# A transformer layer on one core: low weight halves without adding DMAs, modulation at a shorter interval, and one more raw weight buffer

## The chip, the cores and the metric

The kernel runs on one core of one Trainium2 chip. The metric is the device time of one execution in microseconds (us). The core's engines are TensorE (PE in the profile, its weight loads PEld), VectorE (DVE), ScalarE (ACT) and GpSimd (POOL); SyncE (SP) issues most DMAs. Each engine takes its instructions in program order and waits at each for semaphores of others.

## What is computed

One layer of a hybrid model over 512 tokens of width 2048, in float32. Cut to what matters here:

```python
mod = silu(c) @ w_ada + b_ada                      # 2048 x 12288
sh1, sc1, gt1, sh2, sc2, gt2 = split(mod, 6)
h = rms_norm(x, norm1_g) * (1 + sc1) + sh1
proj = h @ w_in                                    # attention and RWKV columns
att_out = dsa_sparse_attention(q, k, v, iq, ik, iw)    # index scores, top-k, softmax
rwkv_out = rwkv7_time_mix(...)                     # a scan over time with a 64 x 64 state per head
x = x + gt1 * (concat([att_out, rwkv_out]) @ w_out)
h2 = rms_norm(x, norm2_g) * (1 + sc2) + sh2
x = x + gt2 * ((silu(h2 @ w_ffn_gate) * (h2 @ w_ffn_up)) @ w_ffn_down)
```

## The kernel before, in words

**Big products.** Every product with a large weight matrix runs in float32r with operands that are split in two: `hi` is the value rounded to float32r, `lo` is what the rounding left. A product is three matmuls of 128 x 128 weights with 512 columns (hi x hi, hi x lo, lo x hi). The weights come in *jobs* (`job`, line 235): one job is one raw chunk `wraw` of up to 512 KB, usually four blocks of 128 rows by 256 columns, and 24 matmuls. Its matmuls write `acc` (or `vacc`) in PSUM.

**Weights on the way.** `issue_to` (line 242) issues the raw load of a job into one of three `wraw` buffers; `run_jobs` (line 272) calls it at the start of job i for the jobs up to i + 2. `split_to` (line 250) turns half a raw chunk at a time into a `whi` and a `wlo` tile of 128 x 512, four buffers of each. At the start of job i the halves of job i + 1 are split, in the middle the first half of job i + 2 may follow. There are two ways to split. The common one, `split` (line 196), is a cast on ScalarE for `whi` and a subtraction on VectorE for `wlo`. In the middle part of the program (`state["mid"]`, from the first job after the first block until the output product) every second half goes another way: the cast on ScalarE, then a second ScalarE instruction that writes -hi into `wlo`, then a DMA on GpSimd's queue that reads the same weights again from memory and adds them onto `wlo`.

**The order of the work.** The program is written by Python generators that run beside each other while the kernel is built. `run_jobs` is the main one; each time it yields, every other stream may write some instructions: the preparation of the RWKV pairs (`prep`, line 657), two triangular solves (`solve`, line 787; the first on GpSimd, the second on VectorE), two scans over time, the index scores and the top-k, the attention heads, and the modulation. A record of estimated engine times, `clk`, decides when a stream may go on: `until(tile)` waits for the estimated time at which a tile is ready, `room("dve", lim)` until VectorE's estimated backlog is at most `lim` us. So a number in such a call sets the order of instructions on all engines, and nothing else does.

**The modulation.** The first two sixths of `mod` are made at the start on TensorE. The other four (`gt1`, `sh2`, `sc2`, `gt2`) come from `ada_stream` (line 974): 16 blocks of 512 columns, each of 16 chunks `wad` of 128 x 512 (256 KB). A chunk is loaded by SP three chunks ahead into a tile of the general pool, and VectorE adds it, scaled, onto the block's sum in one instruction; the first chunk of a block is scaled by ScalarE. A block's sum is then reduced over partitions on VectorE (`ada_sum`, line 1010: a transpose and a reduce). A chunk may be worked on once `PACE` us (line 137) of the estimated time have gone by since the last and VectorE's backlog is under 2.0 us:

```python
            while now() < last + (PACE if bi < 12 else PACE2):
                yield
            yield from until(t)
            yield from room("dve", 2.0)
```

The first 12 blocks, 192 chunks, have to be done before the second norm: `norm2` (its first lines are `while done["ada"] < 12: yield`) writes nothing until then. Then it takes the sum of squares `ssum` through TensorE (`pst`), a power on GpSimd and TensorE's transposes (`prb`), and the first `h2` is made on VectorE and ScalarE. The FFN's products follow.

**The general pool.** `gpool` (line 166) has 29 tiles of 128 x 512 float32, 2 KB per partition each, for all the streams' work, the chunks `wad` included.

Nearly all instructions are recorded by one helper, so that the profile shows them at line 127.

Of the kernel before, what the change touches and what calls it, by code (L numbers as in the profile page):

```python
# [8 lines left out]
F32 = mybir.dt.float32  # L9
F32R = mybir.dt.float32r  # L10
I32 = mybir.dt.int32
AF = mybir.ActivationFunctionType
OP = mybir.AluOpType
# [10 lines left out]
PAIRS = 8  # L24
# [24 lines left out]
def layer_kernel(ctx, tc, x, c, positions, w_ada, b_ada, norm1_g, w_in, q_norm_g, k_norm_g,  # L49
# [38 lines left out]
    class Queue:  # L88
# [3 lines left out]
        def __getattr__(self, op):  # L92
# [3 lines left out]
            def call(*args, **kw):  # L96
# [26 lines left out]
                if key2 != "pe":  # L123
                    for v in vals[1:]:
                        if nm(v) in psread:
# [4 lines left out]
    PE, V, A, P, SP = (Queue(e, k) for e, k in ((nc.tensor, "pe"), (nc.vector, "dve"), (nc.scalar, "act"),  # L130
                                                (nc.gpsimd, "pool"), (nc.sync, "dma")))

    def now():
        return clk["pe"]

    SLACK = 0.5
    PACE, PACE2 = 4.2, 3.0

    def until(*aps):

        t = max(ready.get(nm(a), 0.0) for a in aps) + SLACK
        while now() < t:
            yield

    def room(key="dve", lim=3.0):
        while clk[key] - now() > lim:
            yield
# [15 lines left out]
    hpool = ctx.enter_context(tc.tile_pool(name="hp", bufs=32))  # L163
    wpool = ctx.enter_context(tc.tile_pool(name="wp", bufs=2))
    bpool = ctx.enter_context(tc.tile_pool(name="bp", bufs=6))
    gpool = ctx.enter_context(tc.tile_pool(name="gp", bufs=29))
    spool = ctx.enter_context(tc.tile_pool(name="sp", bufs=8))
    pgp = ctx.enter_context(tc.tile_pool(name="pg", bufs=4, space=PSUM))
    rpool = ctx.enter_context(tc.tile_pool(name="rp", bufs=8))
# [3 lines left out]
    def G(name="g", dt=F32):  # L173
        return gpool.tile([128, 512], dt, name=name, tag="g")
# [18 lines left out]
    def mm(o, l, r, start=True, stop=True):  # L193
        PE.matmul(o, l, r, start=start, stop=stop)

    def split(hi, lo, src, eng=None):
        A.copy(hi, src)
        (eng or V).tensor_tensor(lo, src, hi.bitcast(F32), op=OP.subtract)
# [34 lines left out]
    state = {"issued": 0, "split": 0, "mid": False, "ffn": False}  # L233
# [8 lines left out]
    def issue_to(n, eng=SP):  # L242
        while state["issued"] < min(n, len(jobs)):
            j = jobs[state["issued"]]
            t = wpool.tile([128, 1024], F32, name="wraw", tag="wraw", bufs=3)
            j["raw"] = t[:, 0:j["nk"] * j["n"]].rearrange("p (k m) -> p k m", m=j["n"])
            eng.dma_start(j["raw"], j["view"][:, j["k0"]:j["k0"] + j["nk"], j["c0"]:j["c0"] + j["n"]])
            state["issued"] += 1

    def split_to(n):  # L250
        while state["split"] < min(n, len(subs)):
            j, u = subs[state["split"]]
            if j["i"] >= state["issued"]:
                return
            h = max(1, j["nk"] // 2)
            hi = wpool.tile([128, 512], F32R, name="whi", tag="whi", bufs=4)
            lo = wpool.tile([128, 512], F32R, name="wlo", tag="wlo", bufs=4)
            hv, lv = (t[:, 0:h * j["n"]].rearrange("p (k m) -> p k m", m=j["n"]) for t in (hi, lo))
            if state["mid"] and state["split"] % 2:
                A.copy(hv, j["raw"][:, u * h:(u + 1) * h])  # L260
                A.activation(lv, hv.bitcast(F32), AF.Copy, scale=-1.0)
                P.dma_start(lv, j["view"][:, j["k0"] + u * h:j["k0"] + u * h + h, j["c0"]:j["c0"] + j["n"]],
                            accum_op=OP.add)
            else:
                split(hv, lv, j["raw"][:, u * h:(u + 1) * h])
            j["hi"] += [hv[:, i, :] for i in range(h)]
            j["lo"] += [lv[:, i, :] for i in range(h)]
            state["split"] += 1
# [3 lines left out]
    def run_jobs(a, b, eng=SP, every=3):  # L272
        for i in range(a, b):
            j = jobs[i]
            while j["need"] is not None and not j["need"]():
                yield
            if j["before"] is not None:
                j["before"]()
            issue_to(i + 3, eng)
            split_to(j["s0"] + 4)  # L280
            n = 0
            half = None
            for kk, o, l, r, st, sp in j["mms"](j):
                if half is None and j["nk"] > 1 and kk >= j["nk"] // 2 and not j["whole"]:
                    half = 1
                    split_to(j["s0"] + 5)
                mm(o, l, r, st, sp)
                n += 1
                if n % every == 0:
                    yield  # L290
            if j["after"] is not None:
                j["after"]()
# [63 lines left out]
    done = {"ada1": 0, "prep": 0, "idx": 0, "topk": 0, "ada": 0, "hfree": 0, "rb": 0}  # L356
# [7 lines left out]
    for k1, n1 in BLOCKS:  # L364
        for kind in ("scale", "shift"):
            n = 4 // n1
# [72 lines left out]
    def ccol(k):  # L439
        return cact[:, k:k + 1]  # L440
# [63 lines left out]


    issue_to(3, P)
    V.memset(vr2[:, 0:128], 0.0)
    for t in range(1, NT):
# [465 lines left out]
    def ada_stream():  # L974
        blocks = [(n, o, b) for n, o in (("gt1", 2), ("sh2", 3), ("sc2", 4), ("gt2", 5)) for b in range(4)]
        chunks = [(bi, k) for bi in range(16) for k in range(KD)]
        tiles = {}

        def load(i):
            if i < len(chunks):  # L980
                bi, k = chunks[i]
                n, o, b = blocks[bi]
                t = G("wad")
                SP.dma_start(t, wav[:, k, o * D + b * 512:o * D + b * 512 + 512])
                tiles[i] = t

        nl = 0
        acc = None
        last = 0.0
        for i, (bi, k) in enumerate(chunks):  # L990
            while bi >= 12 and not state["ffn"]:
                yield
            while nl < min(i + 3, 192 if bi < 12 else 256):
                load(nl)
                nl += 1
            t = tiles.pop(i)
            while now() < last + (PACE if bi < 12 else PACE2):
                yield
            yield from until(t)
            yield from room("dve", 2.0)  # L1000
            last = now()
            if k == 0:
                A.activation(t, t, AF.Copy, scale=ccol(0))
                acc = t
                continue
            V.scalar_tensor_tensor(acc, t, ccol(k), acc, op0=OP.mult, op1=OP.add)
            if k == KD - 1:
                start(ada_sum(acc, *blocks[bi]))

    def ada_sum(acc, n, o, b):  # L1010
        yield from until(acc)
        part = parts[o % 2]
        yield from room("dve", 4.0)
        colsum(part[:, b * 16:b * 16 + 16], acc)
        if b < 3:
            return
        yield from until(part)
        yield from banks(1)
        pc = PS("pc")
        spread(pc[:, 0:16], part)  # L1020
        yield
        V.tensor_tensor(mod[n], pc[:, 0:16], v1[:, o * 16:o * 16 + 16], op=OP.add)
        if n == "sc2":
            V.scalar_tensor_tensor(gp2, mod[n], 1.0, v1[:, 112:128], op0=OP.add, op1=OP.mult)
        done["ada"] += 4
# [215 lines left out]
    def start(gen):  # L1241
        streams.append(gen)
# [218 lines left out]
    ada_issue()  # L1461
    drive(until(jobs[1]["raw"]))
    split_to(4)

    def first_need(b):
# [3 lines left out]
    for b in range(len(BLOCKS)):  # L1469
        drive(first_need(b))  # L1470
        if b == 2:
            vectors2()
        drive(run_jobs(2 * b, 2 * b + 2, P if b < len(BLOCKS) - 1 else SP, 3))
# [15 lines left out]
    start(post_stream(range(0, 8, 2)))  # L1489
    start(post_stream(range(1, 8, 2)))  # L1490
    start(ada_stream())
    start(idx_stream())
    start(head_stream())
    start(head_stream())
    start(mixed_stream())
    state["mid"] = True
    drive(run_jobs(nfirst, i_out))
    state["mid"] = False
    drive(run_jobs(i_out, i_norm2))
    split_to(i_norm2 + 2)  # L1500
    drive(norm2())
# [63 lines left out]
```

## Time and profile before

| what | value |
|---|---|
| time, median of 3 runs | 2835.9 us (2832.57 to 2840.85) |
| the profiled execution | 2832.56 us, its span 2830.8 us |
| TensorE busy | 2678.4 us, 95% of the span, mean granted clock 0.970 |
| VectorE busy | 1396.9 us, 49% |
| ScalarE busy | 877.0 us, 31% |
| GpSimd busy | 438.1 us, 15% |
| DMA | 424.76 MB, mean 150 GB/s |

How to read it: the shares are means over parts with different limits. TensorE's granted clock is a share of full speed; its two levels are 2.4 GHz (1.0) and 1.2 GHz (0.5). A wait is named by the engine and the tile it was about to write, then by whom it waited for: "PE acc <- DMA wlo" is TensorE's product `acc` held up by a DMA into `wlo`. A wait for several semaphores is put down to the one that came last. Idle time counts for the end only where it holds up TensorE's chain.

### The profile page before, as it was taken

Reading aid. Unit: us, or ns where it says so; the run is one execution under the profiler, and the core shown is the slowest. Engines: PE = TensorE matmul, PEld = TensorE weight load, DVE = VectorE, ACT = ScalarE, POOL = GpSimd, SP = SyncE. Lnnn points to the kernel's source line nnn. Section 1 sums busy time; section 2 is a strip of 40 time slices with the busy share of each in tenths; the row PEclk is TensorE's granted clock in tenths of the full one; section 3 lists DMA queues with packets and bytes.
Section 4 is the critical chain, followed back from the end, with each engine's and each line's share of the span. In section 5 each row is a group of like instructions: output and inputs, shape, how many; then the busy total and the mean of one; then the engine's idle time right before and its main releaser. Section 6 shows DMA issues by size and latency. Waiting matters only on the chain.

```text
span 2830.8 us, 35243 instructions
## 1 busy us (share of the span) xinstructions
PE 2678.4 (95%) x13343; PEld 2116.4 (75%) x13343; DVE 1396.9 (49%) x2304; ACT 877.0 (31%) x1577; POOL 438.1 (15%) x455
## 2 busy tenths in 40 slices
PE   7989988879999979998699999999999999999999
PEld 4567766657777757887488888888888888888887
DVE  3455555778657876655854533332333323333233
ACT  3244433323332334432332222222222222222222
POOL 2012267851113323210300000000000000000000
PEclk8999999889999989999799999999999999999999
DMA  9987888587867546545454433323333333333333
GB/s 323 308 229 194 208 191 214 149 204 177 222 170 205 130 123 156 158 164 174 135 185 164 156 97 97 97 94 100 97 97 97 97 97 97 97 97 97 97 97 112
DMA packets 411963, 424.76 MB, mean 150 GB/s; under 512 B 55226, under 2 KB 359168, under 8 KB 411792
## 3 DMA queue, kind: packets, MB, share of 16 engines
q1 hardware_dynamic: 381312, 387.78, 44.2%
q0 software_dynamic: 30336, 34.46, 7.6%
q8 instruction: 105, 1.72, 0.2%
q14 instruction: 66, 0.54, 0.1%
q10 hardware_dynamic: 144, 0.26, 0.0%
HBM read 386.77 MB, written 35.65 MB: 149 GB/s over the span
## 4 chain that ended last, share of the span: by engine, by line
PE 79%; DMA 7%; DVE 5%; issue 4%; SPq 2%; ACT 1%; POOL 1%; POOLq 0%; DVEq 0%; ACTq 0%
PE acc L127 68%; DMA wlo<-in_w_in_dram 3%; PE vacc L127 3%; DMA wraw<-in_w_in_dram 2%; PE po L127 2%; SPq L127 2%; PE p L127 2%; PE adaacc L127 1%; DMA wada<-in_w_ada_dram 1%; DVE work L127 1%; PE pl L127 1%; DVE wlo L127 1%; DVE score L127 1%; PE dot L127 0%; DMA xtok<-in_x_dram 0%
## 5 line engine op out<-in xcount | busy, mean ns | idle before, releaser
L127 DVE TENSOR_TENSOR wlo<-wraw,whi 128x512 fp32r<-128x512 f32 (+2 forms) x750 | 517.5, 695 | 1106.8 <-ACT whi L127 1097.5
L127 ACT CAST whi<-wraw 128x512 fp32r<-128x512 f32 (+2 forms) x860 | 518.0, 608 | 1393.6 <-PE acc L127 1200.6
L127 PE MATMUL acc<-hhi,wlo 128*128 128x512 f32 (+1 forms) x2256 | 892.8, 396 | 51.1 <-DMA wlo<-in_w_in_dram 45.7
L127 PE MATMUL acc<-hhi,whi 128*128 128x512 f32 (+1 forms) x2256 | 915.5, 406 | 6.9 <-ACT hhi L127 3.9
L127 PE MATMUL acc<-hlo,whi 128*128 128x512 f32 (+1 forms) x2256 | 888.9, 394 | 3.4 <-DVE hlo L127 3.4
L127 PEld LDWEIGHTS acc<-hhi,wlo 128*128 128x128 f32 (+1 forms) x2256 | 428.3, 190 | 152.3 <-DMA wlo<-in_w_in_dram 52.8
L127 PEld LDWEIGHTS acc<-hhi,whi 128*128 128x128 f32 (+1 forms) x2256 | 428.2, 190 | 127.7 <-issue 28.8
L127 PEld LDWEIGHTS acc<-hlo,whi 128*128 128x128 f32 (+1 forms) x2256 | 428.4, 190 | 96.1 <-DVE hlo L127 6.2
L127 PE MATMUL acc<-act,whi 128*128 128x512 f32 x1408 | 434.9, 390 | 0.0
L127 PEld LDWEIGHTS acc<-act,whi 128*128 128x128 f32 x1408 | 263.2, 188 | 53.9
L127 PE MATMUL acc<-act,wlo 128*128 128x512 f32 x704 | 274.0, 389 | 0.0
L127 POOL DMA_DIRECT2D wlo<-in_w_in_dram x109 | 126.6, 1161 | 451.0 <-ACT wlo L127 359.2
L127 DVE SCALAR_TENSOR_TENSOR wad<-wad,cact 128x512 f32<-128x512 f32 x240 | 195.1, 813 | 1.2
L127 PEld LDWEIGHTS acc<-act,wlo 128*128 128x128 f32 x704 | 132.1, 188 | 27.6
L127 PE MATMUL acc<-mhi,whi 128*128 128x512 f32 x256 | 100.4, 392 | 0.0
L127 PE MATMUL acc<-mhi,wlo 128*128 128x512 f32 x256 | 99.7, 389 | 0.0
L127 PE MATMUL acc<-mlo,whi 128*128 128x512 f32 x256 | 99.6, 389 | 0.0
L127 DVE SCALAR_TENSOR_TENSOR x<-acc,gt,x 128x512 f32<-128x512 f32 x80 | 57.3, 751 | 39.8 <-PE acc L127 39.8
L127 POOL TENSOR_TENSOR stmp<-X,N 128x504 f32<-128x504 f32 (+33 forms) x69 | 71.1, 1031 | 3.3
L127 ACT ACTIVATE wlo<-whi 128x512 fp32r<-128x512 f32 (+1 forms) x110 | 69.2, 629 | 3.5
L127 POOL TENSOR_TENSOR X<-X,stmp 128x504 f32<-128x504 f32 (+33 forms) x69 | 68.8, 997 | 5.4
L127 PE MATMUL vacc<-whi,hhi 128*128 128x512 f32 x128 | 55.1, 430 | 1.8 <-ACT whi L127 1.8
(259 smaller groups left out, 2194.1 us busy)
## 6 DMA issues: line engine op xcount, KB each, us to landing
wad<-in_w_ada_dram SPq DMA_DIRECT2D x256, 256.0 KB, 3.9
wraw<-in_w_in_dram SPq DMA_DIRECT2D x108, 512.0 KB, 5.5
wraw<-in_w_ffn_down_dram SPq DMA_DIRECT2D x88, 512.0 KB, 3.5
wraw<-in_w_ffn_gate_dram SPq DMA_DIRECT2D x84, 512.0 KB, 3.5
wraw<-in_w_ffn_up_dram SPq DMA_DIRECT2D x84, 512.0 KB, 3.5
wada<-in_w_ada_dram SPq DMA_DIRECT2D x128, 256.0 KB, 6.6
wlo<-in_w_in_dram POOLq DMA_DIRECT2D x107, 256.0 KB, 5.4
wraw<-in_w_out_dram SPq DMA_DIRECT2D x32, 512.0 KB, 3.5
```

The lines of the kernel that those rows point to most:

```text
L127: return f(*args, **kw)
```

## The change

All halves are split by the cast on ScalarE and the subtraction on VectorE. There are four raw weight buffers, and at the start of job i the loads up to job i + 3 are issued. The general pool gives up two tiles of 2 KB per partition, which is the size of the fourth raw buffer. The first 12 blocks of the modulation go at an interval of 2.4 us of the estimated time instead of 4.2, and the backlog of VectorE under which a chunk may go is 3.5 us, or 1.5 us between the end of the preparation and the end of the top-k, instead of 2.0.

```diff
-    PACE, PACE2 = 4.2, 3.0
+    PACE, PACE2 = 2.4, 3.0
...
-    gpool = ctx.enter_context(tc.tile_pool(name="gp", bufs=29))
+    gpool = ctx.enter_context(tc.tile_pool(name="gp", bufs=27))
...
-            t = wpool.tile([128, 1024], F32, name="wraw", tag="wraw", bufs=3)
+            t = wpool.tile([128, 1024], F32, name="wraw", tag="wraw", bufs=4)
...
-            if state["mid"] and state["split"] % 2:
-                A.copy(hv, j["raw"][:, u * h:(u + 1) * h])
-                A.activation(lv, hv.bitcast(F32), AF.Copy, scale=-1.0)
-                P.dma_start(lv, j["view"][:, j["k0"] + u * h:j["k0"] + u * h + h, j["c0"]:j["c0"] + j["n"]],
-                            accum_op=OP.add)
-            else:
-                split(hv, lv, j["raw"][:, u * h:(u + 1) * h])
+            split(hv, lv, j["raw"][:, u * h:(u + 1) * h])
...
-            issue_to(i + 3, eng)
+            issue_to(i + 4, eng)
...
-            yield from room("dve", 2.0)
+            yield from room("dve", 1.5 if done["prep"] == PAIRS and not done["topk"] else 3.5)
```

The order of instructions moves on every engine. Three places show how. In the rows `x_...`, `st`, `gt_372`, `gp_376` and the like are tiles of the program, `wlo` and `whi` weight halves, `wad` modulation chunks, `X`, `N` and `stmp` those of the solve.

VectorE at the second norm, from the last update of the residual on, before:

```order
L127 SCALAR_TENSOR_TENSOR x_11167<-acc,gt_372,x_11167 128x512
L127 TENSOR_TENSOR ssum<-ssum,sqx 128x512
L127 SCALAR_TENSOR_TENSOR wad<-wad,cact 128x512 x13
L127 STREAM_TRANSPOSE tr<-wad 128x512
L127 TENSOR_REDUCE part_377<-tr 128x16
L127 SCALAR_TENSOR_TENSOR wad<-wad,cact 128x512 x15
L127 STREAM_TRANSPOSE tr<-wad 128x512
L127 TENSOR_REDUCE part_377<-tr 128x16
L127 TENSOR_TENSOR sc_374<-pc,v_230 128x16
L127 SCALAR_TENSOR_TENSOR gp_376<-sc_374,v_230 128x16
L127 TENSOR_SCALAR st<-pst 128x4
L127 TENSOR_TENSOR hx<-x_9842,prb 128x512
```

and now:

```order
L127 SCALAR_TENSOR_TENSOR x_11168<-acc,gt_372,x_11168 128x512
L127 TENSOR_TENSOR ssum<-ssum,sqx 128x512
L127 TENSOR_SCALAR st<-pst 128x4
L127 TENSOR_TENSOR hx<-x_9947,prb 128x512
L127 TENSOR_SCALAR hx<-hx,gp_376,sh_373 128x512
L127 TENSOR_TENSOR hlo<-hx,hhi 128x512
```

28 modulation steps, two column sums and the two small instructions that need them no longer stand between `ssum` and `st`. Counted against the 10,032 big products, VectorE's last step of the 12th block stood at product 3696, the last ahead of the norm, and now stands at 2827.

VectorE in the preparation of a pair, behind product 1075, before:

```order
L127 TENSOR_SCALAR st<-pst 128x8
L127 SCALAR_TENSOR_TENSOR wad<-wad,cact 128x512
L127 TENSOR_TENSOR wlo<-wraw,whi 128x512
L127 SCALAR_TENSOR_TENSOR wad<-wad,cact 128x512
L127 SCALAR_TENSOR_TENSOR L<-reset,sg 128x512
L127 SCALAR_TENSOR_TENSOR kkn<-k,v_231,prb 128x512
L127 TENSOR_SCALAR kf<-at,v_231,der 128x512
```

and now:

```order
L127 TENSOR_SCALAR st<-pst 128x8
L127 SCALAR_TENSOR_TENSOR wad<-wad,cact 128x512
L127 TENSOR_TENSOR wlo<-wraw,whi 128x512
L127 TENSOR_TENSOR gt_372<-pc,v_230 128x16
L127 SCALAR_TENSOR_TENSOR wad<-wad,cact 128x512
L127 TENSOR_TENSOR wlo<-wraw,whi 128x512
L127 SCALAR_TENSOR_TENSOR wad<-wad,cact 128x512
L127 TENSOR_TENSOR wlo<-wraw,whi 128x512
L127 SCALAR_TENSOR_TENSOR L<-reset,sg 128x512
L127 SCALAR_TENSOR_TENSOR kkn<-k,v_231,prb 128x512
L127 TENSOR_SCALAR kf<-at,v_231,der 128x512
```

Two more adds and one more modulation step stand ahead of `L`, the preparation's running sum. Counted over products 400 to 1000, 1000 to 1600, 1600 to 2600 and 2600 to 3600, VectorE had 26, 25, 42 and 70 adds of low halves and now has 50, 52, 83 and 84; modulation steps were 29, 29, 46 and 44 and now are 50, 51, 57 and 19.

GpSimd in the first solve, before:

```order
L127 TENSOR_TENSOR stmp<-X,N 128x177
L127 TENSOR_TENSOR X<-X,stmp 128x3x59
L127 DMA wlo<-in_w_in_dram 128x2x256
L127 TENSOR_TENSOR stmp<-X,N 128x174
L127 TENSOR_TENSOR X<-X,stmp 128x3x58
L127 TENSOR_TENSOR stmp<-X,N 128x228
L127 TENSOR_TENSOR X<-X,stmp 128x4x57
```

and now:

```order
L127 TENSOR_TENSOR stmp<-X,N 128x177
L127 TENSOR_TENSOR X<-X,stmp 128x3x59
L127 TENSOR_TENSOR stmp<-X,N 128x174
L127 TENSOR_TENSOR X<-X,stmp 128x3x58
L127 TENSOR_TENSOR stmp<-X,N 128x228
L127 TENSOR_TENSOR X<-X,stmp 128x4x57
```

The issue of the adding DMA between two pairs of the solve is gone; there were 110 of them in the program, 25 of them in products 400 to 1000.

## Rows read from the trace of the kernel before

**Rows 1.** The page: TensorE's busy tenths in 40 slices of the span.

```profile
PE   7989988879999979998699999999999999999999
```

**Rows 2.** Stretches: us, their length, each engine's busy time (instructions), clock, DMA share.

```profile
core 0: us, PE busy (x) PEld busy (x) DVE busy (x) ACT busy (x) POOL busy (x), PEclk, DMA share, GB/s
150.00:190.00 40.00, 32.00 (x129) 25.12 (x129) 19.46 (x35) 17.81 (x30) 5.95 (x5) 0.91 0.91 269
190.00:378.00 188.00, 173.25 (x882) 134.35 (x881) 98.73 (x156) 79.14 (x139) 46.98 (x44) 0.96 0.83 207
378.00:605.00 227.00, 192.37 (x911) 141.61 (x910) 150.38 (x168) 80.77 (x150) 175.51 (x179) 0.89 0.72 176
605.00:1042.00 437.00, 404.28 (x2575) 303.87 (x2574) 320.25 (x664) 138.45 (x272) 103.81 (x113) 0.96 0.70 180
1042.00:1313.00 271.00, 268.41 (x1340) 220.85 (x1339) 158.41 (x283) 107.56 (x210) 60.51 (x60) 1.00 0.53 160
1332.00:1378.00 46.00, 14.45 (x51) 10.55 (x50) 37.17 (x50) 7.75 (x14) 7.58 (x6) 0.56 0.47 152
1378.00:2800.00 1422.00, 1416.73 (x6267) 1171.91 (x6267) 527.82 (x782) 387.43 (x642) 14.14 (x10) 1.00 0.34 110
```

**Rows 3.** The chain that ended last: start, us, what, and how many instructions.

```profile
1635.61 1108.61 PE acc L127 x4890
```

**Rows 4.** Waits, whole span: engine and tile, releaser, us in total, times, longest.

```profile
ACT whi L127 <- DMA wraw<-in_w_in_dram: 151.5, 25, 14.1
POOL wlo L127 <- ACT wlo L127: 363.4, 68, 19.6
PE acc L127 <- DMA wlo<-in_w_in_dram: 45.7, 15, 6.8
PE pc L127 <- DVE part L127: 27.2, 1, 27.2
PE acc L127 <- DVE wlo L127: 5.3, 2, 4.7
```

**Rows 5.** TensorE's waits for that DMA in 150 to 190, A, B, C.

```profile
PE acc L127 <- DMA wlo<-in_w_in_dram: 8.0, 2, 6.2
PE acc L127 <- DMA wlo<-in_w_in_dram: 12.1, 4, 6.8
PE acc L127 <- DMA wlo<-in_w_in_dram: 15.9, 5, 5.6
PE acc L127 <- DMA wlo<-in_w_in_dram: 7.1, 3, 6.6
```

**Rows 6.** The timeline at the second norm: start, us, engine, instruction, idle before.

```profile
1336.42 0.69 DVE L127 TENSOR_TENSOR ssum<-ssum,sqx 128x512 f32<-128x512 f32 x1 [0.76 <-ACT sqx L127]
...
1362.23 1.87 PE L127 MATMUL pst<-cst,ssum 128*128 128x1 f32 x8
...
1368.19 0.80 PE L127 MATMUL acc<-hhi,whi 128*128 128x512 f32 x1 [1.63 <-ACT hhi L127]
```

**Rows 7.** The page: groups (busy us, mean ns, idle before), and one of DMA issues.

```profile
L127 DVE TENSOR_TENSOR wlo<-wraw,whi 128x512 fp32r<-128x512 f32 (+2 forms) x750 | 517.5, 695 | 1106.8 <-ACT whi L127 1097.5
L127 POOL DMA_DIRECT2D wlo<-in_w_in_dram x109 | 126.6, 1161 | 451.0 <-ACT wlo L127 359.2
wraw<-in_w_in_dram SPq DMA_DIRECT2D x108, 512.0 KB, 5.5
```

**Rows 8.** VectorE's adds and modulation steps in A, then B, then C.

```profile
L127 DVE SCALAR_TENSOR_TENSOR wad<-wad,cact 128x512 f32<-128x512 f32 x29 | 21.9, 756 | 0.0
L127 DVE TENSOR_TENSOR wlo<-wraw,whi 128x512 fp32r<-128x512 f32 x25 | 17.3, 693 | 66.3 <-ACT whi L127 66.3
L127 DVE SCALAR_TENSOR_TENSOR wad<-wad,cact 128x512 f32<-128x512 f32 x29 | 33.7, 1162 | 0.0
L127 DVE TENSOR_TENSOR wlo<-wraw,whi 128x512 fp32r<-128x512 f32 (+1 forms) x25 | 24.6, 985 | 59.7 <-ACT whi L127 59.6
L127 DVE SCALAR_TENSOR_TENSOR wad<-wad,cact 128x512 f32<-128x512 f32 x47 | 35.7, 759 | 0.2
L127 DVE TENSOR_TENSOR wlo<-wraw,whi 128x512 fp32r<-128x512 f32 x42 | 29.4, 700 | 49.3 <-ACT whi L127 44.0 <-PE acc L127 4.8 <-PE vacc L127 0.3
```

## The prediction, made before the changed kernel was run

> **What bounds the kernel now.** I read the 40 slices first [rows 1]: from slice 20 on TensorE is full, so what can be won lies in the first half. The stretches [rows 2] put numbers on it. From 1378 to 2800 us TensorE is busy for 1416.7 of 1422 us, at full clock; its big products follow each other every 1108.61 / 4890 = 0.227 us [rows 3], so nothing in this change can shorten that part. Ahead of it I name four stretches after the big products (`acc` and `vacc` matmuls) that they hold: A, 190 to 378 us, products 400 to 1000; B, 378 to 605 us, products 1000 to 1600; C, 605 to 1042 us, products 1600 to 2600; D, 1042 to 1313 us, products 2600 to 3600. TensorE is idle for 8.0 us in 150 to 190, 14.8 in A, 34.6 in B, 32.7 in C, 2.6 in D and 31.6 in 1332 to 1378. Where it idles, the granted clock is down too: a mean of 0.89 in B and 0.56 in the last stretch.
>
> Then I asked who is waited for [rows 4]. Two causes stand out. One is the adding DMA that finishes every second low half in the middle part: 45.7 us in 15 waits, 8.0 of it in 150 to 190, 12.1 in A, 15.9 in B, 7.1 in C [rows 5]. The other is one wait of 27.2 us for the last modulation sum before the second norm. A VectorE add of a low half, which takes the DMA's place, is waited for twice, 5.3 us in all. What is left of the idle time in B and C (18.7 and 25.6 us) has other causes, which the change does not touch.
>
> **The change part by part.** *The second norm.* The timeline [rows 6] shows the sum of squares done at 1336.42 + 0.69 = 1337.1 us. VectorE then runs modulation steps, and TensorE starts `pst`, which needs the sum of squares alone, at 1362.23. In the new order VectorE goes from the last `ssum` straight to `st`: the 28 steps between them are gone, since the 192nd chunk now stands at product 2827 of 3696. `pst` can start at about 1337.2, 25.0 us earlier. The rest of the chain (`pst` to the first `acc`, 1368.19 - 1362.23 = 6.0 us) stays. From there to 1378 the products ran at half clock in good part; of those 9.8 us at most 4.9 are lost, and a shorter idle time may give some back. I take 26 us, bounds 25 and 29.
>
> *The adds move to VectorE.* 109 DMA issues of 1161 ns leave GpSimd (127 us), as many scaled copies leave ScalarE, and 110 adds of 695 ns come to VectorE, 76 us [rows 7]. ScalarE is busy for 81 of 227 us in B [rows 2], so it is not on the path. Counted in the two orders, A gets 24 adds and 21 modulation steps more, B 27 and 22, C 41 and 11; D gets 14 adds more and 25 steps fewer. VectorE's prices by stretch are in [rows 8]; a column sum costs two instructions, an estimate of 0.7 us each from the adds.
> - A: 98.7 + 24 x 0.693 + 21 x 0.756 + 2 x 0.7 = 133 us of 188. That fits beside TensorE. The 12.1 us of DMA waits go, and the half clock behind them: a mean of 0.96 is 15 us at half speed, at most 7.5 lost. I take 16, bounds 5 and 20.
> - B: GpSimd runs its triangular solve for most of it (busy 175.5 of 227 us), and the same VectorE instructions are slower than in A: an add 985 against 693 ns, a step 1162 against 756. At B's prices VectorE comes to 150.4 + 27 x 0.985 + 22 x 1.162 + 4 x 0.7 = 205 us; at A's it would be 188. With 205 us on one in-order queue and TensorE waiting for its results, 227 can't shrink much: I take 222 us (VectorE 92% busy), 5 won, though 34.6 are idle. Bounds 216 (95% busy) and 250, which is 205 us at 82%, near the 81% that VectorE reaches in 1332 to 1378, where it is the engine waited for.
> - The Trainium skill, "GPSIMD Engine Reference", section "Key points", speaks against the change here: GpSimd shares its SBUF interfaces with VectorE and contends with VectorE instructions that have two SBUF inputs, which each moved add is. The trace agrees (985 against 693 ns), so the sum goes by 205 us and not by 188.
> - C: 320.3 + 41 x 0.700 + 11 x 0.759 = 357 us of 437, 82%. The 7.1 us of DMA waits go, and some of the half clock; the second half's solve, the top-k and the heads are on VectorE, and the waits for them stay. I take 10, bounds 35 won (the 32.7 idle and a little clock) and 25 lost.
> - D: at A's prices VectorE changes by 14 x 0.693 - 25 x 0.756 = -9 us, and 2.6 us of idle time can go. I take 2, bounds 0 and 3.
> - 150 to 190: 8.0 us of DMA waits. I take 7, bounds 0 and 9.
>
> *The queues.* In A 21 modulation chunks of 256 KB come earlier and 25 adding DMAs of 256 KB go, so transfers do not grow. GpSimd waits 363 us for ScalarE ahead of such issues, 19.6 at the longest [rows 4]; the powers for the norms stand behind those issues in its queue, and come earlier now. On SP each load of a chunk still waits for the tile that an earlier step releases; a step that is late holds up the raw weights behind it, and the fourth raw buffer is there to bridge that.
>
> *The fourth raw buffer.* ScalarE waits 151.5 us for raw weights, 14.1 at the longest [rows 4]. A chunk lasts TensorE 24 x 0.227 = 5.4 us, its load lands after 5.5 [rows 7], and it is issued about a chunk before its first half is cast. One more chunk of lead covers that and part of the 14.1. It is how A and C keep what they win; I count nothing beside it. The two general tiles that pay for it I count at nothing too; one wait for a tile would cost at most about as much as that longest one, 14.1 us.
>
> *Sum*: 26 + 16 + 5 + 10 + 2 + 7 = 66 us. The profiled execution took 2832.56 us (span 2830.8), 3.3 below the median of 2835.9; 2832.6 - 66 gives **2766 us**.
>
> **The rivals.**
> - *VectorE is late for every half.* An add stands in VectorE's queue behind up to 3.5 us of backlog (2.0 before) and the preparation's bursts, and its half is needed about a chunk, 5.4 us, later. B and C hold 52 + 83 = 135 adds. For: 205 of 227 us in B, and the contention. Against: two waits for such adds so far, and VectorE idles 66.3 us in A and 44.0 in C because its adds come early and wait for ScalarE [rows 8]. At a mean wait of 0.7 us per add (the longest so far is 4.7) B and C lose 94 us and win nothing; the other gains are 51, so 2832.6 + 94 - 51 = 2876. It decides against the kernel from 51 / 135 = 0.38 us per add.
> - *Only the norm's wait goes.* The adds on VectorE give back ahead of the norm what the DMA waits cost: 2832.6 - 26 = 2806. For: B's sum. Against: A and 150 to 190 have room on VectorE.
> - *TensorE is kept fed.* The upper bounds of all parts, B's by VectorE's 205 us: 29 + 20 + 11 + 35 + 3 + 9 = 107, giving 2726. For: the raw weights come a chunk earlier everywhere. Against: 25.6 us of C's idle time is not the DMAs'.
> - That the shorter interval does not do what it says can be left out: in the new order the modulation ends 869 products before the norm, 197 us at 0.227, and would have to slip by all that.
>
> **How the numbers follow.** Forecast 0.50, only the norm 0.22, TensorE fed 0.19, VectorE late 0.09. The range goes from below the fed case, 2708 (C's half clock, 0.04 x 437 = 17 us at most, given back as well), to 2816, past the norm-only case. A measurement of this kernel tells a difference from about 0.3%, 8.5 us. Faster: 0.50 + 0.19 + 0.18 of the norm-only case = 0.87; its other 0.04 (the stretches ahead lose most of what the norm wins) is within 0.3%; slower 0.09.
>
> **What would show it.** Right: no wait of 27 us for the modulation sum, and `pst` within 2 us of `ssum`; no waits for a DMA into `wlo`; products 1000 to 1600 in some 220 us with VectorE 88 to 95% busy and adds near 1 us; waits for VectorE's `wlo` of 10 to 30 us in all; a clock of 0.98 or more in A. Wrong: over 50 us of waits for VectorE's `wlo` (the first rival), B under 205 us (the contention costs less than the rows say), or ScalarE still waiting over 100 us for raw weights.

## The result and the profile after

The changed kernel takes **2755.2 us** (median of 4 runs, 2751.61 to 2756.23), the kernel before 2836.7 beside it: a ratio of 0.971, 95% interval 0.9693 to 0.9728, 81.5 us less. The profiled execution took 2751.61 us; all rows of after come from it.

The page of after: busy times of the engines, and TensorE's 40 slices, to be held against [rows 1].

```profile
PE 2662.3 (97%) x13343; PEld 2105.4 (77%) x13343; DVE 1460.1 (53%) x2414; ACT 808.2 (29%) x1467; POOL 332.3 (12%) x346
PE   7999988889999899998999999999999999999999
```

The slices from 20 on were full and are; what changed lies ahead of them. Stretches of after, cut at the same big products as A, B, C and D, columns as in [rows 2]:

```profile
186.00:352.20 166.20, 166.20 (x882) 131.40 (x881) 130.93 (x206) 64.62 (x115) 19.26 (x19) 1.00 0.71 223
352.20:566.30 214.10, 186.98 (x917) 138.14 (x916) 182.84 (x217) 68.37 (x129) 163.50 (x160) 0.94 0.66 190
566.30:982.50 416.20, 398.38 (x2548) 298.83 (x2548) 350.23 (x715) 110.11 (x225) 54.73 (x62) 0.98 0.58 170
982.50:1254.90 272.40, 271.16 (x1367) 223.66 (x1366) 149.42 (x275) 98.90 (x199) 49.58 (x51) 1.00 0.36 116
```

In A TensorE has no idle time left and its clock is at the upper level throughout. In B it still idles for 27.1 us, in C for 17.8. Counted between the same big products, in us (the n-th record of `acc` or `vacc` in each trace):

| products | before | after | difference | forecast |
|---|---|---|---|---|
| start to 400 | 189.9 | 186.0 | -3.9 | -7 |
| A, 400 to 1000 | 188.0 | 166.2 | -21.8 | -16 |
| B, 1000 to 1600 | 226.8 | 214.1 | -12.7 | -5 |
| C, 1600 to 2600 | 437.7 | 416.2 | -21.5 | -10 |
| D, 2600 to 3600 | 270.6 | 272.4 | +1.8 | -2 |
| norm, 3600 to 4000 | 137.6 | 114.0 | -23.6 | -26 |
| 4000 to 10000 | 1366.9 | 1366.9 | 0 | 0 |

The waits of after over the whole span, columns as in [rows 4]:

```profile
ACT whi L127 <- DMA wraw<-in_w_in_dram: 25.9, 6, 5.8
PE pT L127 <- DVE work L127: 17.5, 4, 5.9
PE pst L127 <- DVE sums L127: 11.6, 4, 5.4
PE acc L127 <- DVE wlo L127: 7.7, 5, 3.1
PE pst L127 <- DVE ssum L127: 2.4, 1, 2.4
```

Three rows of [rows 4] have no counterpart any more: GpSimd's wait for ScalarE's `wlo`, TensorE's for the DMA into `wlo`, and TensorE's for `part`. The row to look at twice is the first: ScalarE waits 25.9 us for raw weights, where it waited 151.5. The timeline at the second norm, against [rows 6]:

```profile
1278.38 0.69 DVE L127 TENSOR_TENSOR ssum<-ssum,sqx 128x512 f32<-128x512 f32 x1 [0.76 <-ACT sqx L127]
...
1279.22 1.02 PE L127 MATMUL pst<-cst,ssum 128*128 128x1 f32 x8 [2.38 <-DVE ssum L127]
...
1283.88 0.80 PE L127 MATMUL acc<-hhi,whi 128*128 128x512 f32 x1 [1.62 <-ACT hhi L127]
```

`ssum` ends at 1279.07 and `pst` starts 0.15 us later; it was 25.1 us. The groups of the page that answer to [rows 7]:

```profile
L127 DVE TENSOR_TENSOR wlo<-wraw,whi 128x512 fp32r<-128x512 f32 (+2 forms) x860 | 603.8, 707 | 1038.9 <-ACT whi L127 1032.1
wraw<-in_w_in_dram SPq DMA_DIRECT2D x107, 512.0 KB, 5.5
```

### The profile page after: what moved, and what is told of

Same layout as the page of the kernel before. It is cut to its first block, busy times and chain, and to the rows that moved or that the text cites. A ratio compares the mean times of both kernels' runs of the same rounds, so it can differ in the third digit from the quotient of the medians.

```text
span 2749.8 us, 35166 instructions
## 1 busy us (share of the span) xinstructions
PE 2662.3 (97%) x13343; PEld 2105.4 (77%) x13343; DVE 1460.1 (53%) x2414; ACT 808.2 (29%) x1467; POOL 332.3 (12%) x346
## 4 chain that ended last, share of the span: by engine, by line
PE 87%; DVE 5%; DMA 3%; POOL 2%; issue 1%; SPq 1%; ACT 1%; DVEq 0%; POOLq 0%; ACTq 0%
PE acc L127 74%; PE vacc L127 3%; PE p L127 2%; PE po L127 2%; SPq L127 1%; DVE wlo L127 1%; PE adaacc L127 1%; DVE wad L127 1%; DMA wada<-in_w_ada_dram 1%; POOL stmp L127 1%; POOL X L127 1%; PE pl L127 1%; DVE hx L127 1%; PE dot L127 1%; PE pA L127 0%
## 5 line engine op out<-in xcount | busy, mean ns | idle before, releaser
L127 DVE TENSOR_TENSOR wlo<-wraw,whi 128x512 fp32r<-128x512 f32 (+2 forms) x860 | 603.8, 707 | 1038.9 <-ACT whi L127 1032.1
L127 DVE SCALAR_TENSOR_TENSOR x<-acc,gt,x 128x512 f32<-128x512 f32 x80 | 57.3, 751 | 45.4 <-PE acc L127 45.4
L127 PEld LDWEIGHTS acc<-mhi,wlo 128*128 128x128 f32 x256 | 48.0, 188 | 10.0
L127 PEld LDWEIGHTS acc<-mlo,whi 128*128 128x128 f32 x256 | 48.1, 188 | 9.9
L127 PEld LDWEIGHTS acc<-mhi,whi 128*128 128x128 f32 x256 | 48.1, 188 | 9.8
```

Of the source, the lines that this page charges most:

```text
L127: return f(*args, **kw)
```

## The experiments

The change has three parts: S, all halves split on VectorE (no adding DMAs); R, a fourth raw buffer with loads one chunk further ahead, paid for with two general tiles; M, the modulation's interval and backlog. The theory after the result: S and M do what the prediction says, and R, which the sum counted at nothing, is worth some 30 us, because ScalarE's wait for raw weights all but vanished. The rival: R does nothing, and S and M are worth more than their terms. Each kernel below was timed against the kernel before, which took 2831.4 to 2837.5 us beside them; the times are medians. Where two of these kernels lie close together, the ratios count and not the times. "The new lead" is that of the change, loads up to job i + 3; "the old lead" ends at job i + 2.

**S alone.** The kernel before with the change's `split_to` and nothing else:

```diff
-            if state["mid"] and state["split"] % 2:
...
+            split(hv, lv, j["raw"][:, u * h:(u + 1) * h])
```

> Only the split of the change: no adding DMA, every add on VectorE; interval, raw buffers and general tiles as before. Theory one: the waits for the adding DMA and the half clock behind them go, 40 to 50 us, about 2790 us; the wait before the second norm stays near 25 us. Rival, the raw weights were what was late and the adding DMA only stood behind them: ScalarE still waits over 100 us for raw weights, and the time is 2820 us or above.

Measured 2817.1 us, ratio 0.993 (0.9909 to 0.9951). Its waits for raw weights and at the norm stand as before:

```profile
ACT whi L127 <- DMA wraw<-in_w_in_dram: 143.7, 29, 15.1
PE pc L127 <- DVE part L127: 28.0, 1, 28.0
```

A falls to 175.4 and B to 214.5 us, but C rises from 437.7 to 457.2. S wins and gives a good part of it back in C. The time is far from the 2790 us of the first theory and 3 under the rival's bound; the 143.7 us of waits for raw weights are as the rival said.

**M alone.** The kernel before with the interval and the backlog of the change:

```diff
-    PACE, PACE2 = 4.2, 3.0
+    PACE, PACE2 = 2.4, 3.0
...
-            yield from room("dve", 2.0)
+            yield from room("dve", 1.5 if done["prep"] == PAIRS and not done["topk"] else 3.5)
```

> Only the modulation's interval and backlog limits of the change; adding DMAs, three raw buffers and 29 general tiles as before. Theory one, the gains add up: the 27 us wait for the last modulation sum goes and nothing else, about 2836 - 25 = 2811 us, with 45 us of TensorE waits for the adding DMA as before. Rival, the parts need each other: the modulation steps that move ahead slow the stretches with the adding DMAs, and the time stays at 2825 us or above.

Measured 2823.7 us, ratio 0.9952 (0.9937 to 0.9968): 13.8 us less, where the norm alone (products 3690 to 3696) falls from 34.9 to 9.0. That lies between the two expectations. B rises from 226.8 to 243.7: the additional steps stand beside the solve there, and TensorE still waits for the adding DMAs, 35.4 us over the whole span.

**S and R, without M.** The changed kernel with the interval 4.2 and the backlog 2.0 of before:

```diff
-    PACE, PACE2 = 2.4, 3.0
+    PACE, PACE2 = 4.2, 3.0
...
-            yield from room("dve", 1.5 if done["prep"] == PAIRS and not done["topk"] else 3.5)
+            yield from room("dve", 2.0)
```

> The change without its modulation part: no adding DMA and four raw buffers, interval 4.2 and limit 2.0 as before. Theory one: the changed kernel's 2755 us plus the 25 us wait before the second norm, less some 3 us for a lighter VectorE ahead of it, about 2777 us. Rival: the stretches of the solve shrink by more than 15 us because VectorE has fewer steps there, and the time is 2765 us or below.

Measured 2786.9 us, ratio 0.9822 (0.9799 to 0.9845), 30 us under S alone and above both expectations: the norm holds 22.4 us more than in the changed kernel (31.0 against 8.6), which was expected, and C takes 439.6, which was not. Two of its waits:

```profile
ACT whi L127 <- DMA wraw<-in_w_in_dram: 15.7, 3, 6.1
PE pc L127 <- DVE part L127: 23.3, 1, 23.3
```

**S and M, without R.** The changed kernel with three raw buffers, loads up to job i + 2 and 29 general tiles:

```diff
-    gpool = ctx.enter_context(tc.tile_pool(name="gp", bufs=27))
+    gpool = ctx.enter_context(tc.tile_pool(name="gp", bufs=29))
...
-            t = wpool.tile([128, 1024], F32, name="wraw", tag="wraw", bufs=4)
+            t = wpool.tile([128, 1024], F32, name="wraw", tag="wraw", bufs=3)
...
-            issue_to(i + 4, eng)
+            issue_to(i + 3, eng)
```

> The change without its raw buffer: no adding DMA, modulation at 2.4, but three raw buffers, loads one chunk less ahead, 29 general tiles. Theory one: the fourth buffer bridges a little, about 2755 + 10 = 2765 us. Rival, the raw weights are the cause: ScalarE waits over 100 us for them again, TensorE waits for ScalarE's or VectorE's halves, 2785 us or above.

Measured 2792.1 us, ratio 0.9838 (0.9816 to 0.986): 36.8 us above the changed kernel, with ScalarE waiting 187.3 us for raw weights, as the expectation's rival said. So R is worth 30 to 37 us beside S, M is worth 25 to 32, and R is no smaller than the other two. The rival that R does nothing falls.

**Buffer or lead.** The changed kernel, four raw buffers and 27 general tiles, but the loads are issued as far ahead as before:

```diff
-            issue_to(i + 4, eng)
+            issue_to(i + 3, eng)
```

> The changed kernel with its four raw buffers and 27 general tiles, but loads issued to job i + 2 as before. Theory one, what the fourth buffer brings is the lead of one more chunk: ScalarE waits 140 us or more for raw weights as in the run without the buffer, about 2787 to 2792 us. Rival, it is the free buffer that counts, since SP no longer stands at a load whose buffer is not yet released: within 8 us of the changed kernel's 2755.

Measured 2793.6 us, ratio 0.9863 (0.9846 to 0.988), the time of S and M without R. A free buffer alone does nothing, and two general tiles fewer cost nothing that can be told from noise: in the two traces VectorE, ScalarE and GpSimd have their instructions in the same order, SP its DMAs, and TensorE all but 14 of its 13343. What counts is the lead, as the first theory had it. The stretches A, B and C of this kernel, columns as in [rows 2], and its wait for raw weights:

```profile
179.00:356.70 177.70, 169.39 (x882) 132.55 (x881) 123.89 (x198) 61.88 (x113) 17.62 (x19) 0.99 0.62 191
356.70:584.00 227.30, 192.31 (x918) 140.20 (x917) 181.28 (x219) 67.17 (x128) 159.05 (x160) 0.91 0.64 183
584.00:1020.80 436.80, 406.63 (x2547) 306.48 (x2546) 350.76 (x713) 110.69 (x228) 56.53 (x63) 0.95 0.55 159
```

```profile
ACT whi L127 <- DMA wraw<-in_w_in_dram: 186.0, 32, 15.8
PE acc L127 <- ACT whi L127: 8.5, 2, 5.4
```

Against the rows of after, A, B and C together lose 45.3 us and TensorE's idle time in them falls from 73.5 to 44.9; the rest is clock (0.99, 0.91, 0.95 against 1.00, 0.94, 0.98). TensorE's wait that names ScalarE's `whi` is only 8.5 us of it; the other 20 us of idle time went from waits with other names. For A the trace shows where they come from. With the old lead TensorE idles 8.3 us there and waits for `work`, `sums` and `pack`, tiles of the preparation, which VectorE and ScalarE make. Some 10 us ahead of each of the three waits for VectorE, VectorE idles for 8.5, 8.3 and 5.3 us at an add of a low half, because ScalarE's cast waits for raw weights; the preparation stands behind that add. One such place, in order of time:

```profile
248.87 1.14 ACT L127 CAST whi<-wraw 128x512 fp32r<-128x512 f32 x2 [9.26 <-DMA wraw<-in_w_in_dram]
249.52 0.69 DVE L127 TENSOR_TENSOR wlo<-wraw,whi 128x512 fp32r<-128x512 f32 x1 [8.45 <-ACT whi L127]
251.40 1.22 DVE L127 TENSOR_TENSOR_SCAN L<-reset,sg 128x512 f32<-128x512 f32 x1
258.96 0.44 PE L127 MATMUL pT<-cst,work 128*128 128x128 f32 x2 [2.48 <-DVE work L127]
```

The lead also changes the order of the instructions, which could be a cause by itself. For A that can be set aside: in all eight kernels here with the new lead from the second block on, A takes 166.1 to 166.2 us and TensorE has no idle time, whether 31 or 51 modulation steps stand in it; in the three with all adds on VectorE and the old lead (S alone, S and M, this one) A takes 175.4 to 177.7. For B and C it stays open how much of the gain is the weights' doing.

**The lead at the start.** The first 288 products take 129.0 us in the changed kernel. With the new lead at the start they take 127.8 to 130.7 in the five kernels that have it, with the old one 120.5 to 123.5 in the eight others. So one kernel has the old lead in the first block of products only:

```diff
-            issue_to(i + 4, eng)
+            issue_to(i + (3 if i < nfirst else 4), eng)
```

> The changed kernel with loads to job i + 2 in the first block of jobs and to i + 3 from then on. In the four runs with four raw buffers and a lead of four the first 288 products took 129 us, in the runs with three 121 to 122. Theory one, the extra lead takes transfer time from the first modulation's loads where the DMA engines are full: 122 us again and about 2755 - 7 = 2748 us. Rival, the order of the streams there is what differs, by chance: still 127 us or more, 2755 us.

Measured 2739.6 us, ratio 0.9675 (0.9658 to 0.9691), 15.6 us under the changed kernel by the times and 10 by the ratios. The first 288 products take 122.4 us, which is 6.6 of it, as the first theory said; B is 2.0 shorter, C 8.1 (408.1 against 416.2), and D gives 4.5 back. By which path the added lead costs time in the first block wasn't settled.

**An interval between the two.** The changed kernel with `PACE` 3.2:

```diff
-    PACE, PACE2 = 2.4, 3.0
+    PACE, PACE2 = 3.2, 3.0
```

> The changed kernel with the interval 3.2 instead of 2.4; by its order the 12th block still ends some 250 products before the second norm, and products 1000 to 1600 hold about 10 modulation steps fewer. Theory one, VectorE's load sets the length of those products: 5 to 10 us less there, about 2747 us. Rival, only the norm's wait hangs on the interval: within 3 us of the changed kernel's 2755.

Measured 2761.4 us, ratio 0.9746 (0.9725 to 0.9767). The interval only just meets that of the changed kernel (0.9693 to 0.9728), and neither theory gave such a time. A and the norm are as with 2.4, B is 212.2, C 429.8. The norm's wait is gone at 3.2 already; 7 steps fewer in B shorten it by 2 us, and C gives more than that back.

**What sets B.** In the first solve, GpSimd's instructions with two inputs are replaced by copies with one input of the same sizes. This kernel leaves out the first solve's result:

```diff
-                E.tensor_tensor(t3, X3[:, a:b, j:j + 1].broadcast_to(sh), row.broadcast_to(sh), op=OP.mult)
-                E.tensor_tensor(X3[:, a:b, j + 1:C], X3[:, a:b, j + 1:C], t3, op=OP.add)
+                if g:
+                    E.tensor_tensor(t3, X3[:, a:b, j:j + 1].broadcast_to(sh), row.broadcast_to(sh), op=OP.mult)
+                    E.tensor_tensor(X3[:, a:b, j + 1:C], X3[:, a:b, j + 1:C], t3, op=OP.add)
+                else:
+                    E.tensor_scalar(t3, row.broadcast_to(sh), 1.0, 0.0, op0=OP.mult, op1=OP.add)
+                    E.tensor_scalar(X3[:, a:b, j + 1:C], t3, 1.0, 0.0, op0=OP.mult, op1=OP.add)
```

> The changed kernel with the first solve's two-input instructions on GpSimd replaced by scaled copies with one input, the same number in the same places (the first solve's result is left out). Theory one, contention for the memory interface sets VectorE's price in products 1000 to 1600 and VectorE's load sets their length: an add falls from 985 to about 700 ns, a modulation step from 1080 to about 760, and those products take 190 to 200 us and not 214, in all about 2735 to 2742 us. Rival, the preparation's chain sets the length: prices fall but the products still take 210 us or more, 2752 us or above. Second rival, GpSimd's instructions contend whatever their inputs: the prices stay near 1000 ns.

Measured 2715.0 us, ratio 0.9588 (0.9567 to 0.961). First the rows of after in B, VectorE's steps and adds, then those of this kernel, its stretch B and its wait for `work`, the tile that the preparation makes on VectorE and TensorE transposes:

```profile
L127 DVE SCALAR_TENSOR_TENSOR wad<-wad,cact 128x512 f32<-128x512 f32 x49 | 52.9, 1080 | 4.4 <-DMA wad<-in_w_ada_dram 4.3
L127 DVE TENSOR_TENSOR wlo<-wraw,whi 128x512 fp32r<-128x512 f32 (+1 forms) x50 | 49.2, 985 | 24.1 <-ACT whi L127 24.0
```

```profile
350.50:548.60 198.10, 181.44 (x933) 136.52 (x932) 149.69 (x227) 67.90 (x127) 107.79 (x160) 0.97 0.82 229
L127 DVE SCALAR_TENSOR_TENSOR wad<-wad,cact 128x512 f32<-128x512 f32 x47 | 39.8, 847 | 6.6 <-DMA wad<-in_w_ada_dram 6.6
L127 DVE TENSOR_TENSOR wlo<-wraw,whi 128x512 fp32r<-128x512 f32 (+1 forms) x49 | 38.7, 792 | 26.5 <-ACT whi L127 26.4
PE pT L127 <- DVE work L127: 5.3, 2, 4.1
```

B is 16 us shorter, within the first theory's 190 to 200, though an add falls to 792 ns and not to 700. The wait for `work` falls from 17.5 to 5.3 us; C is 27.8 shorter, and D 8.8 longer. GpSimd's solve also got shorter (107.8 us busy in B against 163.5). For an add the trace tells its price and the length of the solve apart: the adds of B that overlap no GpSimd instruction take 689 ns in the changed kernel (10 of 50) and 688 here (15 of 49), those that overlap one 1059 and 838 (means). For the length of B the two aren't told apart. On the mean the adds are still dearer than the 693 ns of A [rows 8]. The Trainium skill, "SBUF — State Buffer", section "Who interferes with whom", says that a VectorE instruction with two SBUF inputs contends with a GpSimd instruction that reads SBUF. The runs agree: with GpSimd instructions that read one input an add takes 792 ns.

**Fewer steps in B.** The changed kernel with an interval of 6.0 while the first solve runs:

```diff
-            while now() < last + (PACE if bi < 12 else PACE2):
+            while now() < last + (PACE2 if bi >= 12 else 6.0 if done["prep"] >= 4 and 0 not in solved else PACE):
```

> The changed kernel with the interval 6.0 while GpSimd's solve is being written and 2.4 otherwise; by its order products 1000 to 1600 hold 27 modulation steps instead of 51 and the 12th block still ends some 400 products before the norm. Theory one: 24 steps of 1.08 us are 26 us less on VectorE there, the products take 195 to 202 us and not 214, about 2740 us. Rival, the preparation's chain sets the length: 210 us or more there, within 4 us of 2755.

Measured **2730.3 us** (2729.58 to 2733.8), ratio 0.9642 (0.962 to 0.9665): 24.9 us under the changed kernel by the times and 19 by the ratios, the shortest time here of a kernel that computes the whole layer. Its stretch B:

```profile
354.80:559.40 204.60, 183.02 (x918) 137.47 (x917) 157.21 (x192) 67.53 (x127) 159.22 (x160) 0.95 0.59 165
PE pT L127 <- DVE work L127: 15.6, 3, 5.9
```

VectorE has 25.6 us less to do in B, and B shrinks by 9.5, less than the 12 to 19 of the first theory and more than the rival allows. C shrinks by 18.4, from 416.2 to 397.8, though the steps that B no longer holds come later; D grows by 5.1.

**Both, and a longer pause.** The last two kernels put the interval of 6.0 beside the old lead at the start; the second keeps it up to the end of the top-k, with `not done["topk"]` in place of `0 not in solved`.

> Both edits that are thought to win: lead of three in the first block, interval 6.0 while GpSimd's solve is being written. If they add up, 2730 - 7 = 2723 us. If the first products stay at 129 us, 2730.

> As the run with both edits, but the interval 6.0 lasts until the end of the top-k; by its order products 1600 to 2600 hold 37 modulation steps instead of 56 and the 12th block ends some 240 products before the second norm. Theory one, VectorE's load still sets some of the length of those products: 19 steps of 0.76 us are 14 us less on VectorE, 5 to 10 us won there, about 2715 us. Rival, the scan's and the heads' chains set the length: within 4 us of the run with both edits, or slower where the steps that come later stand ahead of the heads.

Measured 2744.4 us, ratio 0.969 (0.9676 to 0.9705), and 2746.3, ratio 0.9702 (0.9682 to 0.9722). Neither is clear of noise from the changed kernel, where 2723 and 2715 us were expected. The gains do not add. A is 166.2 in both and B 203.9 and 204.6, as with the interval alone, and the start is won (123.5 and 122.2). But C takes 420.4 and 433.7. Over the eleven kernels of this section C runs from 388.4 to 457.2 us. Any edit ahead of it reorders the attention heads, the second solve and the top-k in it, and a difference of some 15 us between two orders there can't be credited to the edit's purpose. That holds for the gains above too: of what R, the start and the longer interval win, 17 to 21, 8 and 18 us lie in C.

**Not tried.** R without S. What R is worth beside the adding DMAs is not known.

## Why the prediction was right, and where it was not

The time, 2755.2 us, lies in the range and 10.8 under the forecast; the change is faster, as said. The norm's wait and those for the adding DMAs went as argued. That the sum came near is in part luck: S and M without R win 45.4 us (2837.5 - 2792.1) and R another 36.8, where the forecast had 66 for all and nothing for R beyond keeping what the others win. Step by step:

*The second norm: right.* 25 us were forecast between `ssum` and `pst`, and the gap fell from 25.1 to 0.15. S with R but without M keeps the wait for `part`, 23.3 us; M alone loses it. The 26.3 us between products 3690 and 3696 come less 2.7 behind, so 23.6 of the forecast 26 remain.

*A: mechanism right, size beyond its bound.* -21.8 us against -16 (bounds -5 to -20). Not only the DMA waits and the clock behind them went; all 14.8 us of idle time did. With the old lead A takes 177.7, which is 10.3 of it; the other 11.5 us are the lead's.

*B: the term failed, to the good side.* "205 us on one in-order queue" was to hold B at 222. VectorE was busy for 182.8 us, 85% and not the 88 to 95% that were to show it right, and B took 214.1, under the lower bound of 216. The price of an add held, 985 ns in both kernels, and a step fell from 1162 to 1080. What didn't hold is that all else keeps its time: VectorE's other instructions in B, 150.4 - 33.7 - 24.6 = 92.1 us for 114 before, took 182.8 - 52.9 - 49.2 = 80.7 for 118 (more on this in the last section). VectorE's load sets B only in part: taking 25.6 us of it away shortened B by 9.5. The 188 us held against the 205 have only the added instructions at A's prices; with all adds and steps at A's prices the same sum gives some 169. The lead has 13.2 us of B: with the old one B takes 227.3, so there S and M together win nothing, and the prediction's caution held for these two.

*C: direction right, size off.* -21.5 against -10, inside the bounds; 20.6 us is the distance to the kernel with the old lead. In S alone C lost 19.5 us, inside the lower bound too. The prediction left 25.6 us of C's idle time to causes "which the change does not touch"; 17.8 are idle now. With C's scatter over orders no finer account of it holds.

*The start: half.* -3.9 against -7. Without the added lead, products 0 to 400 take 148.6 us against 158.3 before, so the DMA waits went as said and more; the added lead costs 6.3 us in the first block. The prediction named no price for raw loads that go ahead of others.

*The fourth raw buffer: the step that failed.* "I count nothing beside it" was wrong by 30 to 38 us. I took the buffer to cover other gains. ScalarE's 151.5 us of waits for raw weights were in [rows 4], but TensorE's own waits for `whi` came to 3.1 us in the kernel before, so I read them as idle time of an engine that isn't the bottleneck:

```profile
PE vacc L127 <- ACT whi L127: 1.8, 1, 1.8
PE acc L127 <- ACT whi L127: 1.3, 1, 1.3
```

In the kernel with the old lead it is 8.5 us, and yet the lead is worth 38.3. VectorE's 66.3 us of idle time in A, which wait for `whi` [rows 8], were read as room, because its adds "come early"; in the kernel with the old lead the preparation stands behind such an add, and TensorE behind the preparation.

*The sum* came out 15.5 us short (81.5 against 66): A, B and C won 25 us beyond their terms, and the start, D and the norm took 9 back. With the old lead A, B and C win 10.7 us, where 31 were forecast; the lead's 45.3 there make up for that and more.

*The rivals.* VectorE late for every half: TensorE waited for its `wlo` 5 times, 7.7 us in all, over 860 adds, and less than the 10 to 30 us expected; it would have decided from 0.38 us per add over the 135 of B and C. Only the norm: S and R alone win 50 us without it. TensorE fed (2726) came true in A, and not in B and C.

## What to carry to other kernels

A wait of an engine that isn't the bottleneck, for loads, is not always free: ask what stands behind it in program order, on that engine and on the one that takes its result, and whether the bottleneck needs that. If the load lands as late as the chunk lasts (here 5.5 us against 5.4), try one more chunk of lead by itself, and test lead and buffer apart: the buffer without an earlier issue gave nothing. Where a table of estimated times sets the order, measure edits in pairs before adding their gains, and take a stretch with the scatter of C as a band, not as a number.

## What the runs showed of the hardware

An add on VectorE beside GpSimd's solve took 985 ns with two-input instructions on GpSimd and 792 with one-input ones, against 693 in A and 700 in C [rows 8], where GpSimd is busy for a quarter of the time [rows 2]. The count of such adds and steps in B went from 54 to 99, and the time of the solve's instructions on GpSimd hardly moved: its two kinds of instruction, first before and then after, in the groups of the whole span:

```profile
L127 POOL TENSOR_TENSOR stmp<-X,N 128x504 f32<-128x504 f32 (+33 forms) x69 | 71.1, 1031 | 3.3
L127 POOL TENSOR_TENSOR X<-X,stmp 128x504 f32<-128x504 f32 (+33 forms) x69 | 68.8, 997 | 5.4
```

```profile
L127 POOL TENSOR_TENSOR stmp<-X,N 128x504 f32<-128x504 f32 (+33 forms) x69 | 70.8, 1026 | 44.5 <-DMA N<-nab 37.4 <-DVE work L127 1.4 <-DVE wad L127 1.3
L127 POOL TENSOR_TENSOR X<-X,stmp 128x504 f32<-128x504 f32 (+33 forms) x69 | 72.0, 1043 | 5.4
```

139.9 us became 142.8. So on GpSimd's side the contention was not twice as much with nearly twice the instructions. VectorE's other instructions in B became cheaper, and that goes with the adding DMAs, which GpSimd issues: such an instruction takes 881 and 872 ns on the mean in the two kernels that have them (before, M alone) and 769 to 809 in the ten that have none and solve with two-input instructions, among 114 to 121 such instructions in each. By which path the issues make them dearer isn't shown.
